# An encoder block whose up-projection weight sums are made ahead for ten of twenty-two channels instead of all

## The chip, the core and the metric

The kernel runs on one core of one Trainium2 chip. The metric is the device time of one launch in microseconds (us), the median of three runs. A profiled execution gives the trace. The engines are TensorE (PE, with its weight loads as PEld), VectorE (DVE), ScalarE (ACT), GpSimd (POOL) and SyncE (SP), which here issues every transfer from one queue.

## What is computed

Two sequences of 512 tokens, width 1024, all float32, go through one layer:

```python
h = _rmsnorm(x, g_attn) * (1 + sc1) + sh1
z = h @ w_in                        # q, k, v of mixer A; low-rank q, kv of mixer B; two gates
oa = _window_attention(qa, ka, va, sink_a)          # mixer A: window of +-128, 8 heads on 2 kv heads
# mixer B: dense attention, 8 heads, low-rank q and kv
mix = jax.nn.sigmoid(gla) * (oa @ w_o_a) + jax.nn.sigmoid(glb) * (ob @ w_o_b)
x = x + gt1 * (mix @ w_out)
h2 = _rmsnorm(x, g_ffn) * (1 + sc2) + sh2
u = _dwconv(h2 @ w_up, conv_w, conv_b)              # D_FF = 2816, so w_up is 1024 x 5632
ua, ug = jnp.split(u, 2, axis=-1)
x = x + gt2 * ((jax.nn.silu(ug) * ua) @ w_down)
```

## The kernel before

Each float32 operand of a matmul is split in two float32r parts, `hi` (a cast) and `lo` (the operand minus `hi`), and a product is three matmuls: hi by hi, hi by lo, lo by hi. One engine casts and the same or another subtracts; the subtraction reads two tensors from SBUF. Instructions stand on each engine in an order that a scheduler writes out when the program is built, and an engine takes them in that order: an instruction that waits holds all behind it. `tc.keep_in_program_order` pins an instruction of a helper among its engine's others.

The program's stages are: projections and preparation (0 to 225 us); the two attention mixers, B first and then A, with the gate projections filled in between (225 to 600); the output projection with the gated sum (600 to 800); the up-projection with convolution and gating (807 to 1215); the down-projection (to the end).

**Mixers.** A list of 128 units, 64 of mixer B (`PairB`) and then 64 of mixer A (`GroupA`), is walked in steps. A step issues the scores of one unit and five matmuls of the gate projection (`fill(5)`, `psg` in L495), and three steps later the transposes of that unit's softmax rows. The softmax (L530 to L540) goes DVE maximum, ACT exponential, DVE reciprocal, POOL scaling by `l` (L539); PE transposes the scaled `p` (L545). POOL also splits the gate weights (`wg`). A finished gate tile is copied by ACT to `go` (two buffers) and stored to `gate_d`.

**Weight sums.** The up-projection multiplies the two sequences with a Strassen-like scheme. `w_up` comes in 22 channels, each of four quarters, 128 x 512, which are called a1, a2 (the first half of the rows) and g1, g2 (the second half) here. Seven products per channel are made with the weights a1, a2, g2 and four sums of quarters. `weight_sums` runs one piece per step of the mixers: it loads half a channel (`wsum`, 512 KB, two buffers, L514), makes four POOL additions (L522 to L526) and stores the four sums to `su_d` in memory (L528). There are 44 such pieces, three steps each, over both mixers.

**Up-projection loop.** For each channel, `wraw` loads a quarter or a stored sum (256 KB, seven buffers, L764); `split_w` (L956 to L960) casts on ACT (L958) and subtracts on DVE or POOL (L959) into `wt` (eight buffers). The seven products are 12 matmuls each (L980), in the order a1 by `h1` into px; a2 by `h2` into pz; then the sums into px (`t2`), py (`t1`), px (`t3`), py (`e2`); and g2 into px (`t4`). ACT copies px after the first product and after `t2` and `t3`, and py after `t1` (L985); a product that adds to a bank waits for the copy of what was in it. `conv1` runs one ACT instruction (L991) and two on DVE (L992, L994) into `tmp_u`, four times a channel; `gated` (L999 to L1001) stores the result to `g_d`. The first convolution of a channel writes a `tmp_u` whose last content must have landed in `g_d`. SP issues loads and these stores in one order.

Of the kernel before, what the change touches and what calls it, by code (L numbers as in the profile page):

```python
# [8 lines left out]
F32 = mybir.dt.float32  # L9
# [9 lines left out]
S = 512  # L19
# [12 lines left out]
GW = 4 * AD + 2 * AD  # L32
FF = 2816
NP = FF // 128
EPS = 1e-6
BIG = -1e30

# [2 lines left out]
def encoder_block(ctx, tc, x, c_t, w_ada0, b_col, w_ada, b_ada, cols, w_z, w_g, gains, tabs, sink,  # L40
                  w_uq, w_ukv, w_o, w_out, w_up, conv, w_down, out):
    nc = tc.nc
    V, A, G, PE, SY = nc.vector, nc.scalar, nc.gpsimd, nc.tensor, nc.sync
# [7 lines left out]
    o_d = dram.tile([NB, 8, 128, S], F32, name="o_d")  # L51
    g_d = dram.tile([NB, NP, 128, S], F32, name="g_d")
    x1_d = dram.tile([TOK, D], F32, name="x1_d")
    gt_d = dram.tile([2, NB, D], F32, name="gt_d")
    su_d = dram.tile([NP, 128, 4, 512], F32, name="su_d")

# [5 lines left out]
    a1 = const.tile([128, KD, NB], F32, name="a1")  # L62
    a2 = const.tile([128, KD, NB], F32, name="a2")
# [5 lines left out]
    def split_pool(hi, lo, raw, in_order=False):  # L69
        ins = G.tensor_scalar(out=hi, in0=raw, scalar1=1.0, scalar2=0.0, op0=ALU.mult, op1=ALU.add)  # L70
        if in_order:
            tc.keep_in_program_order(ins)
        G.tensor_sub(lo, raw, hi.bitcast(F32))  # L73
# [21 lines left out]
    def mean_eps(a, ss, n):  # L95
        V.tensor_scalar(out=a, in0=ss, scalar1=1.0 / n, scalar2=EPS, op0=ALU.mult, op1=ALU.add)

# [21 lines left out]
    def hblk(name, shape=None, dt=F32R):  # L119
        return hp.tile(shape or [128, KD, S], dt, name=name, tag="h")  # L120
# [7 lines left out]
    with ExitStack() as st:  # L128
# [184 lines left out]
        with ExitStack() as s0:  # L313
# [140 lines left out]
            for _ in mods:  # L454
                pass

    mp = ctx.enter_context(tc.tile_pool(name="mp", bufs=1))

    def mblk(name, tag, shape=None, dt=F32R):
        return mp.tile(shape or [128, KD, S], dt, name=name, tag=tag, bufs=2)  # L460


    with ExitStack() as st:
        gw = st.enter_context(tc.tile_pool(name="gw", bufs=1, side="right"))
# [6 lines left out]
        def gates():  # L471

            ws = []

            def load():
                n = len(ws)
                if n < 2 * KD:
                    w = gw.tile([128, 2, KD, 128], F32R, name="wg", bufs=3)
                    raw = gw.tile([128, KD, 128], F32, name="wg_raw", bufs=2)
                    SY.dma_start(raw, w_g[n // 2, :, n % 2])  # L480
                    for k in range(0, KD, 4):
                        split_pool(w[:, 0, k:k + 4], w[:, 1, k:k + 4], raw[:, k:k + 4])
                    ws.append(w)

            load()
            load()
            for n in range(2 * KD):
                f, m = divmod(n, 2)
                for b in range(NB):
                    if b:  # L490
                        load()
                    ps = psg.tile([128, S], F32, name="psg")
                    for k in range(KD):
                        for i, (wl, hl) in enumerate(((0, h_hi), (0, h_lo), (1, h_hi))):
                            PE.matmul(ps, lhsT=ws[n][:, wl, k, :], rhs=hl[b][:, k, :],  # L495
                                      start=k == 0 and i == 0, stop=k == KD - 1 and i == 2)
                            yield
                    go = gw.tile([128, S], F32, name="go", bufs=2)
                    A.copy(go, ps)
                    SY.dma_start(gate_d[b, f, :, m], go)  # L500

        def weight_sums():

            pin = tc.keep_in_program_order
            halves = [(c, slice(256 * q, 256 * (q + 1))) for c in range(NP) for q in range(2)]
            ts = {}

            def load(n):  # L510
                if n < len(halves):
                    c, cs = halves[n]
                    ts[n] = gw.tile([128, 4, 256], F32, name="wsum", bufs=2)
                    pin(SY.dma_start(ts[n], w_up[c].rearrange("m q p n -> p (m q) n")[:, :, cs]))  # L514

            load(0)
            yield
            yield
            for n, (c, cs) in enumerate(halves):
                t = ts[n]  # L520
                load(n + 1)
                pin(G.tensor_add(t[:, 3], t[:, 2], t[:, 3]))  # L522
                pin(G.tensor_sub(t[:, 2], t[:, 0], t[:, 2]))
                yield
                pin(G.tensor_sub(t[:, 0], t[:, 3], t[:, 0]))
                pin(G.tensor_sub(t[:, 1], t[:, 1], t[:, 0]))  # L526
                yield
                pin(SY.dma_start(su_d[c, :, :, cs], t))  # L528
                yield

        def softmax(ps, n, plen):

# [86 lines left out]
        for j in range(2):  # L619
            n = 1 - 2 * j  # L620
# [91 lines left out]

        blocks = [PairB(b, g) for b in range(NB) for g in range(BH // 2)] + [GroupA(b, g) for b in range(NB) for g in range(AKV)]
        gate = gates()
        wsum = weight_sums()

        def fill(n):
            for _ in range(n):
# [43 lines left out]
    def wraw(src):  # L762
        r = wp.tile([128, 512], F32, name="wraw", bufs=7)
        SY.dma_start(r, src)  # L764
        return r

    def wtile():
        return wp.tile([128, 2, 512], F32R, name="wt", bufs=8)
# [17 lines left out]
    with ExitStack() as s0:  # L786
        wk = s0.enter_context(tc.tile_pool(name="wko", bufs=2))
        ob = []
        raws = [mblk("o_raw0", "st", dt=F32), hblk("o_raw1", dt=F32)]
# [63 lines left out]
    with ExitStack() as s0:  # L853
        wk = s0.enter_context(tc.tile_pool(name="wkx", bufs=1))

        def tmp(tag):
            return wk.tile([128, S], F32, name=f"tmp_{tag}", bufs={"cc": 6, "sf": 4}.get(tag, 2))
# [94 lines left out]

        cw = wk.tile([128, 2 * NP, 4], F32, name="cw")
        SY.dma_start(cw, conv)

        def split_w(raw, lo_eng):  # L956
            w = wtile()
            A.copy(w[:, 0], raw)  # L958
            lo_eng.tensor_sub(w[:, 1], raw, w[:, 0].bitcast(F32))  # L959
            return w.rearrange("p a (k n) -> p a k n", k=4)  # L960

        def weights_first(c):
            for q in range(2):
                yield split_w(wraw(w_up[c, 0, q]), G)

        def weights_rest(c):

            for q, eng in ((0, V), (3, V), (2, V), (1, G)):
                yield split_w(wraw(su_d[c, :, q]), eng)
            yield split_w(wraw(w_up[c, 1, 1]), G)  # L970

        def weights_all(c):
            yield from weights_first(c)
            yield from weights_rest(c)

        def product(ps, w, name, add=False, sl=slice(0, S)):
            for i in range(4):
# [10 lines left out]
        def conv1(c, m, src):  # L988
            cc = c + m * NP
            u = tmp(f"u{m}")  # L990
            A.activation(u, src, AF.Identity, scale=cw[:, cc, 1:2], bias=cw[:, cc, 3:4])  # L991
            V.scalar_tensor_tensor(out=u[:, 1:S], in0=src[:, 0:S - 1], scalar=cw[:, cc, 0:1], in1=u[:, 1:S],  # L992
                                   op0=ALU.mult, op1=ALU.add)
            V.scalar_tensor_tensor(out=u[:, 0:S - 1], in0=src[:, 1:S], scalar=cw[:, cc, 2:3], in1=u[:, 0:S - 1],  # L994
                                   op0=ALU.mult, op1=ALU.add)
            return u
# [54 lines left out]

        for c in range(NP):
            if c < EARLY:
                rest(c, weights_rest(c), *started[c])
            else:
                w = weights_all(c)
                if c == NP - 1:
                    rest(c, w, *first(w), [lambda k=k: down_step(0, k) for k in (1, 2)])
                else:
                    rest(c, w, *first(w))  # L1060
                if c == NP - 2:
                    down_step(0, 0)


    with ExitStack() as s0:
        wk = s0.enter_context(tc.tile_pool(name="wke", bufs=2))
        LATE = 3
        for b in range(NB):
# [22 lines left out]
            for i in range(NT):  # L1091
                t = b * NT + i
                xt = wk.tile([128, D], F32, name="xe", bufs=3)
                SY.dma_start(xt, x1_d[t * 128:(t + 1) * 128, :])
                for hf in range(2):
                    products(i, NP - LATE, NP, (hf,))
                    cs = slice(hf * 512, (hf + 1) * 512)
# [71 lines left out]
```

## Time and profile before

| | |
|---|---|
| median of 3 runs | 1458.52 us (1457.64 to 1461.35) |
| profiled execution, its own time | 1463.69 us |
| its span, first to last instruction | 1461.9 us |
| PE busy | 1395.4 us, 95% of the span |
| DVE, ACT, POOL busy | 64%, 46%, 42% |
| memory read, written | 186.67 MB, 67.13 MB |
| mean granted TensorE clock | 0.989 |

A matmul of 128 x 512 is recorded with about 389 ns but issues every 227 ns, since they are pipelined; busy time is that of the union. The granted clock is a share of full speed. An idle time is put down to what ended it.

### The profile page before, as it was taken

The numbers are of one execution on the slowest core, as the hardware profiler recorded it, in microseconds if no ns is written. First come the engines' busy times: TensorE is split into PE (matmuls) and PEld (weight loads), VectorE is DVE, ScalarE is ACT, GpSimd is POOL, SyncE is SP. The second block draws the span as 40 slices with busy tenths as digits, with TensorE's granted clock in tenths as the row PEclk, the third lists the DMA queues.
The fourth block names the chain that finished last, engine by engine and source line by source line (L and its number), as shares of the span: only waits on it lengthen the run. The fifth ranks groups of instructions, "written<-read, shape, count | busy, mean of one in ns | idle before, by whom it ended". The sixth has DMA issues, their size and how long they took to land.

```text
span 1461.9 us, 21179 instructions
## 1 busy us (share of the span) xinstructions
PE 1395.4 (95%) x7184; PEld 1155.7 (79%) x7184; DVE 941.7 (64%) x1885; ACT 679.5 (46%) x1385; POOL 609.0 (42%) x702
## 2 busy tenths in 40 slices
PE   5888997999999899999998999999999999999998
PEld 4777776888878787787887888888888887888887
DVE  4788774666668786564369776666666668347433
ACT  3475223666666566332136765555555554212210
POOL 3175023676677787455003232222222235444430
PEclk9999999999999999999999999999999999999999
DMA  8565764666666667855432344444434447646522
GB/s 320 195 209 178 239 234 159 196 227 202 227 198 220 208 212 250 286 174 177 143 115 80 108 130 130 125 127 123 130 123 127 132 122 250 205 140 222 185 80 72
DMA packets 162620, 255.19 MB, mean 175 GB/s; under 512 B 21192, under 2 KB 86984, under 8 KB 159440
## 3 DMA queue, kind: packets, MB, share of 16 engines
q1 hardware_dynamic: 162512, 253.84, 53.2%
q8 instruction: 57, 0.93, 0.3%
q14 instruction: 51, 0.42, 0.1%
HBM read 186.67 MB, written 67.13 MB: 174 GB/s over the span
## 4 chain that ended last, share of the span: by engine, by line
PE 78%; DVE 10%; DMA 5%; POOL 3%; ACT 2%; issue 2%; SPq 0%; ACTq 0%; POOLq 0%; DVEq 0%
PE px L980 15%; PE psg L495 9%; PE py L980 8%; PE psd L80 5%; PE psd L81 5%; PE psd L82 5%; PE pz L980 4%; PE ppt L545 3%; PE ppo L608 2%; PE psx L82 2%; PE psx L81 2%; PE psx L80 2%; PE psz L80 1%; PE psz L82 1%; PE psz L81 1%
## 5 line engine op out<-in xcount | busy, mean ns | idle before, releaser
L959 POOL TENSOR_TENSOR wt<-wraw,wt 128x512 fp32r<-128x512 f32 x88 | 119.4, 1363 | 395.4 <-ACT wt L958 362.9
L980 PE MATMUL px<-t,wt 128*128 128x512 f32 x792 | 190.0, 389 | 1.7 <-ACT tmp_cc L985 1.7
L980 PEld LDWEIGHTS px<-t,wt 128*128 128x128 f32 x792 | 148.5, 188 | 33.1 <-ACT tmp_cc L985 2.4
L495 PE MATMUL psg<-h_hi,wg 128*128 128x512 f32 x512 | 172.1, 401 | 0.0
L77 DVE TENSOR_TENSOR wd<-wraw,wd 128x512 fp32r<-128x512 f32 x88 | 96.3, 1133 | 90.8 <-ACT wd L76 90.8
L80 PE MATMUL psd<-wd 128*128 128x512 f32 x352 | 137.0, 389 | 0.1
L82 PE MATMUL psd<-wd 128*128 128x512 f32 x352 | 136.9, 389 | 0.0
L81 PE MATMUL psd<-wd 128*128 128x512 f32 x352 | 136.9, 389 | 0.0
L76 ACT CAST wd<-wraw 128x512 fp32r<-128x512 f32 x88 | 50.8, 619 | 151.5 <-issue 112.7
L958 ACT CAST wt<-wraw 128x512 fp32r<-128x512 f32 x154 | 93.9, 619 | 39.7 <-POOL wt L959 26.5
L495 PEld LDWEIGHTS psg<-h_hi,wg 128*128 128x128 f32 x512 | 97.0, 192 | 18.7 <-POOL wg L73 0.8
L539 POOL TENSOR_SCALAR p<-p,l 128x512 f32<-128x512 f32 (+2 forms) x128 | 78.3, 615 | 63.7 <-DVE l L538 45.9
L495 PE MATMUL psg<-h_lo,wg 128*128 128x512 f32 x256 | 102.7, 401 | 0.0
L537 ACT ACTIVATE p<-pps,nm 128x512 f32<-128x512 f32 (+2 forms) x128 | 78.1, 610 | 39.2 <-DVE nm L534 31.3
L992 DVE SCALAR_TENSOR_TENSOR tmp_u<-tmp_cc,cw,tmp_u 128x511 f32<-128x511 f32 x66 | 57.2, 867 | 41.5 <-ACT tmp_u L991 41.4
L70 POOL TENSOR_SCALAR wd<-wraw 128x512 fp32r<-128x512 f32 x44 | 33.6, 764 | 112.5 <-PE psd L82 84.9
L80 PEld LDWEIGHTS psd<-wd 128*128 128x128 f32 x352 | 66.1, 188 | 14.3 <-issue 0.5
L82 PEld LDWEIGHTS psd<-wd 128*128 128x128 f32 x352 | 66.1, 188 | 13.8
L81 PEld LDWEIGHTS psd<-wd 128*128 128x128 f32 x352 | 66.1, 188 | 13.5
L534 DVE TENSOR_REDUCE nm<-pps 128x1 f32<-128x512 f32 (+2 forms) x128 | 74.7, 584 | 3.2 <-PE pps L82 1.5
L545 PE MATMUL ppt<-ident,p 128*128 128x128 f32 x416 | 66.9, 274 | 8.2 <-POOL p L539 8.2
L73 POOL TENSOR_TENSOR wd<-wraw,wd 128x512 fp32r<-128x512 f32 x44 | 73.1, 1661 | 3.7
(256 smaller groups left out, 3425.7 us busy)
## 6 DMA issues: line engine op xcount, KB each, us to landing
w_ada<-in_w_ada_dram SPq DMA_DIRECT2D x24, 1024.0 KB, 5.5
wsum<-in_w_up_dram SPq DMA_DIRECT2D x44, 512.0 KB, 3.9
su_d<-wsum SPq DMA_DIRECT2D x44, 512.0 KB, 3.6
wraw<-su_d SPq DMA_DIRECT2D x88, 256.0 KB, 3.1
wraw<-in_w_down_dram SPq DMA_DIRECT2D x88, 256.0 KB, 3.2
wraw<-in_w_up_dram SPq DMA_DIRECT2D x66, 256.0 KB, 2.7
g_d<-tmp_u SPq DMA_DIRECT2D x44, 256.0 KB, 2.4
wraw<-g_d SPq DMA_DIRECT2D x44, 256.0 KB, 3.5
```

What stands on the lines that cost most here:

```text
L77: V.tensor_sub(lo, raw, hi.bitcast(F32))
L80: PE.matmul(ps, lhsT=lh, rhs=rh, start=first, stop=False)
L81: PE.matmul(ps, lhsT=lh, rhs=rl, start=False, stop=False)
L82: PE.matmul(ps, lhsT=ll, rhs=rh, start=False, stop=last)
L495: PE.matmul(ps, lhsT=ws[n][:, wl, k, :], rhs=hl[b][:, k, :], start=k == 0 and i == 0, stop=k == KD - 1 and i == 2)
L534: V.tensor_reduce(nm, ps[:, :n], op=ALU.max, axis=AX.X, negate=True)
L537: A.activation(p[:, :n], ps[:, :n], AF.Exp, bias=nm, accum_out=l)
L539: G.tensor_scalar(out=p[:, :plen], in0=p[:, :plen], scalar1=l, scalar2=1.0, op0=ALU.mult, op1=ALU.mult)
L545: PE.transpose(pt[:, j * 128:(j + 1) * 128], p[:, j * 128:(j + 1) * 128], ident)
L958: A.copy(w[:, 0], raw)
L959: lo_eng.tensor_sub(w[:, 1], raw, w[:, 0].bitcast(F32))
L980: PE.matmul(ps[:, sl], lhsT=w[:, wl, i], rhs=h[:, hl, sl], start=not add and i == 0 and n == 0, stop=i == 3 and n == 2, skip_group_check=add)
```

## The change

The sums of the first ten channels (`SUMMED = 10`) are still made during the mixers, in 20 pieces of three steps; there are three `wsum` buffers instead of two, and a piece's store is issued after the additions of the next piece. The second `go` buffer is gone. For the channels 10 to 21 no sum is made ahead or stored: the loop loads a2, g1, g2 beside a1, and POOL makes the four sums in SBUF from them (`tmp_sf`, four buffers that exist already), one channel at a time; DVE subtracts for all four (before: for three, POOL for the fourth).

```diff
+    quarters = [(c, 128 * q) for c in range(SUMMED) for q in range(4)]
+    def weight_sums(tile, width, count, ahead):
...
+        while n < len(loaded):
+            t, dst = loaded[n]
+            n += 1
+            load()
+            pin(G.tensor_add(t[:, 3], t[:, 2], t[:, 3]))
+            pin(G.tensor_sub(t[:, 2], t[:, 0], t[:, 2]))
+            yield
+            pin(G.tensor_sub(t[:, 0], t[:, 3], t[:, 0]))
+            pin(G.tensor_sub(t[:, 1], t[:, 1], t[:, 0]))
+            yield
+            if summed:
+                pin(SY.dma_start(*summed))
+            summed = (dst, t)
+            yield
...
-                    go = gw.tile([128, S], F32, name="go", bufs=2)
+                    go = gw.tile([128, S], F32, name="go", bufs=1)
...
-        wsum = weight_sums()
+        wsum = weight_sums(lambda: gw.tile([128, 4, 256], F32, name="wsum", bufs=3), 256, 2 * SUMMED, 1)
...
+        def weights_rest(c, raws=None):
+            if c < SUMMED:
+                for q, eng in ((0, V), (3, V), (2, V), (1, G)):
+                    yield split_w(wraw(su_d[c, :, q]), eng)
+                yield split_w(wraw(w_up[c, 1, 1]), G)
+                return
+            a1, a2 = raws
+            g1, g2 = wraw(w_up[c, 1, 0]), wraw(w_up[c, 1, 1])
+            sf = [tmp("sf") for _ in range(4)]
+            G.tensor_add(sf[0], g1, g2)
+            G.tensor_sub(sf[1], sf[0], a1)
+            yield split_w(sf[1], V)
+            yield split_w(sf[0], V)
+            G.tensor_sub(sf[2], a1, g1)
+            yield split_w(sf[2], V)
+            G.tensor_sub(sf[3], a2, sf[1])
+            yield split_w(sf[3], V)
+            yield split_w(g2, G)
```

The rows below are the built program's order, engine by engine; line numbers differ between the two files (L539 is L554 after the change, L764 is L779, L959 is L974, L1001 is L1032). POOL at the start of mixer A, before:

```order
L539 TENSOR_SCALAR p<-p,l 128x512 x3
L522 TENSOR_TENSOR wsum<-wsum 128x256
L523 TENSOR_TENSOR wsum<-wsum 128x256
L539 TENSOR_SCALAR p<-p,l 128x512
L525 TENSOR_TENSOR wsum<-wsum 128x256
L526 TENSOR_TENSOR wsum<-wsum 128x256
L70 TENSOR_SCALAR wg<-wg_raw 128x512 x2
L73 TENSOR_TENSOR wg<-wg_raw,wg 128x512
L539 TENSOR_SCALAR p<-p,l 128x256
L73 TENSOR_TENSOR wg<-wg_raw,wg 128x512
```

and the same place after the change:

```order
L554 TENSOR_SCALAR p<-p,l 128x512 x4
L71 TENSOR_SCALAR wg<-wg_raw 128x512 x2
L74 TENSOR_TENSOR wg<-wg_raw,wg 128x512
L554 TENSOR_SCALAR p<-p,l 128x256
L74 TENSOR_TENSOR wg<-wg_raw,wg 128x512
L554 TENSOR_SCALAR p<-p,l 128x384 x2
```

The additions no longer stand between the scalings; the gate weights' splits still do. POOL has no other rows in the mixers that differ in kind.

POOL in the loop at a late channel, where before it held `wt` subtractions alone (82 in a row, four per channel), after the change:

```order
L991 TENSOR_TENSOR tmp_sf<-wraw 128x512
L992 TENSOR_TENSOR tmp_sf<-tmp_sf,wraw 128x512
L995 TENSOR_TENSOR tmp_sf<-wraw 128x512
L997 TENSOR_TENSOR tmp_sf<-wraw,tmp_sf 128x512
L974 TENSOR_TENSOR wt<-wraw,wt 128x512 x3
```

The four sums are those of one channel; the three subtractions behind them are g2 of the channel before it and a1, a2 of the channel itself. POOL's instructions per channel go from four to seven.

SP in the loop at a late channel, one channel's period, before:

```order
L764 DMA wraw<-in_w_up_dram 128x512
L764 DMA wraw<-su_d 128x512 x4
L764 DMA wraw<-in_w_up_dram 128x512 x2
L1001 DMA g_d<-tmp_u_10761 128x512
L1001 DMA g_d<-tmp_u_10808 128x512
```

and after:

```order
L779 DMA wraw<-in_w_up_dram 128x512 x4
L1032 DMA g_d<-tmp_u_10914 128x512
L1032 DMA g_d<-tmp_u_10958 128x512
```

Four loads stand between two channels' stores instead of seven. PE's order is the same in both programs.

## Rows read from the trace of the kernel before

**Rows 1.** Busy time by stretch: start:end, length, PE, PEld, DVE, ACT, POOL (instructions), PE clock, DMA share, GB/s.

```profile
225.00:430.00 205.00, 202.01 (x1065) 167.99 (x1064) 129.42 (x258) 124.33 (x265) 130.56 (x178) 0.99 0.61 201
430.00:592.00 162.00, 151.88 (x832) 127.77 (x832) 122.98 (x371) 99.83 (x259) 120.65 (x179) 0.98 0.69 223
600.00:612.00 12.00, 9.69 (x40) 7.46 (x41) 5.81 (x8) 6.60 (x11) 4.72 (x5) 1.00 0.94 347
815.00:1187.00 372.00, 372.00 (x1642) 308.00 (x1641) 246.06 (x329) 210.06 (x344) 106.43 (x80) 1.00 0.44 131
```

**Rows 2.** PE's waits, 425 to 612 us: who waited for whom, total, times, longest.

```profile
PE ppt L545 <- POOL p L539: 8.2, 5, 3.4
PE ppo L608 <- ACT p L547: 1.5, 1, 1.5
PE psy L82 <- POOL wo L73: 0.9, 1, 0.9
PE psy L80 <- POOL wo L70: 0.8, 1, 0.8
PE psy L80 <- POOL wo L73: 0.8, 1, 0.8
```

**Rows 3.** Chain that ended last, near 490 us: start, duration, what.

```profile
485.53 0.74 POOL wsum L526
...
486.28 3.37 DMA su_d<-wsum
...
489.66 5.93 DMA wsum<-in_w_up_dram
...
497.23 0.49 POOL p L539
...
497.76 0.44 PE ppt L545 x2
```

**Rows 4.** The same chain near 432 us and from 575 us on.

```profile
431.94 5.62 DMA lda<-qa_d
...
575.86 4.81 DMA wsum<-in_w_up_dram
...
589.44 3.84 DMA o_d<-o
...
593.35 2.82 DMA wo_raw<-in_w_o_dram
...
601.48 7.24 DMA wo_raw<-in_w_o_dram
```

**Rows 5.** Busy time by stretch behind the two longest waits (columns of Rows 1).

```profile
498.60:502.10 3.50, 3.50 (x13) 3.00 (x12) 2.02 (x7) 0.49 (x2) 2.13 (x4) 0.51 1.06 388
...
583.90:587.40 3.50, 3.50 (x13) 3.02 (x12) 0.42 (x1) 1.41 (x3) 3.26 (x5) 0.51 0.44 150
```

**Rows 6.** DMA issues in mixer A, 430 to 592 us: count, KB each, median us to landing.

```profile
su_d<-wsum SPq DMA_DIRECT2D x23, 512.0 KB, 3.9
wsum<-in_w_up_dram SPq DMA_DIRECT2D x22, 512.0 KB, 3.7
...
gate_d<-go SPq DMA_DIRECT2D x15, 256.0 KB, 4.2
```

**Rows 7.** Tile `go` in the same stretch: ns min/median/max, first and last start.

```profile
L499 ACT COPY go<-psg x15: 576/587/598, 433.5 to 588.9; 128x512 f32<-128x512 f32 x15
...
DMA to landing us min/median/max: 3.3/4.2/8.3
```

**Rows 8.** The loop near 911 us in order of time: start, duration, engine, line, what [idle before].

```profile
910.95 2.88 PE L980 MATMUL px<-h,wt 128*128 128x512 f32 x12
...
921.83 2.88 PE L980 MATMUL px<-t,wt 128*128 128x512 f32 x12
...
913.27 1.35 POOL L959 TENSOR_TENSOR wt<-wraw,wt 128x512 fp32r<-128x512 f32 x1 [2.81 <-ACT wt L958]
916.49 1.29 POOL L959 TENSOR_TENSOR wt<-wraw,wt 128x512 fp32r<-128x512 f32 x1 [1.86 <-ACT wt L958]
...
914.05 1.13 DVE L994 SCALAR_TENSOR_TENSOR tmp_u<-tmp_cc,cw,tmp_u 128x511 f32<-128x511 f32 x1
...
919.79 0.75 DVE L994 SCALAR_TENSOR_TENSOR tmp_u<-tmp_cc,cw,tmp_u 128x511 f32<-128x511 f32 x1
920.46 0.69 DVE L959 TENSOR_TENSOR wt<-wraw,wt 128x512 fp32r<-128x512 f32 x1
...
915.81 1.18 SPq L1001 DMA_DIRECT2D g_d<-tmp_u  x2
...
918.16 0.82 ACT L991 ACTIVATE tmp_u<-tmp_cc,cw 128x512 f32<-128x512 f32 x1 [0.91 <-DMA g_d<-tmp_u]
```

**Rows 9.** The last channel: PE's wait, then SP's and ACT's rows before it.

```profile
PE px L980 <- ACT tmp_cc L985: 1.7, 1, 1.7
...
1205.90 0.93 SPq L1001 DMA_DIRECT2D g_d<-tmp_u  x2
...
1208.00 0.81 ACT L991 ACTIVATE tmp_u<-tmp_cc,cw 128x512 f32<-128x512 f32 x1 [2.58 <-DVE wd L77]
```

**Rows 10.** A DVE instruction between two of POOL, near 871 us.

```profile
870.78 1.78 DVE L994 SCALAR_TENSOR_TENSOR tmp_u<-tmp_cc,cw,tmp_u 128x511 f32<-128x511 f32 x1
```

More of the change, by code (lines that the diff above doesn't have):

```diff
@@ L34 @@
 NP = FF // 128
+SUMMED = 10
 EPS = 1e-6
@@ L455, in encoder_block, with load @@
                 pass
+    quarters = [(c, 128 * q) for c in range(SUMMED) for q in range(4)]
+    def weight_sums(tile, width, count, ahead):
+        pin = tc.keep_in_program_order
+        loaded = []
+        def load():
+            if len(loaded) < count and quarters:
+                c, c0 = quarters[0]
+                del quarters[:width // 128]
+                t, cs = tile(), slice(c0, c0 + width)
+                pin(SY.dma_start(t, w_up[c].rearrange("m q p n -> p (m q) n")[:, :, cs]))
+                loaded.append((t, su_d[c, :, :, cs]))
+        for _ in range(ahead):
+            load()
+        yield
+        yield
+        n, summed = 0, None
+        while n < len(loaded):
+            t, dst = loaded[n]
+            n += 1
+            load()
+            pin(G.tensor_add(t[:, 3], t[:, 2], t[:, 3]))
[3 more added lines that the diff above has]
+            pin(G.tensor_sub(t[:, 1], t[:, 1], t[:, 0]))
+            yield
+            if summed:
+                pin(SY.dma_start(*summed))
+            summed = (dst, t)
+            yield
+        if summed:
+            yield
+            yield
+            pin(SY.dma_start(*summed))
     mp = ctx.enter_context(tc.tile_pool(name="mp", bufs=1))
@@ L497, in gates @@
                             yield
-                    go = gw.tile([128, S], F32, name="go", bufs=2)
+                    go = gw.tile([128, S], F32, name="go", bufs=1)
                     A.copy(go, ps)
                     SY.dma_start(gate_d[b, f, :, m], go)
[L504 to L529, printed above, removed]
         def softmax(ps, n, plen):
@@ L964, in weights_first @@
                 yield split_w(wraw(w_up[c, 0, q]), G)
[L966 to L970, printed above, removed]
+        def weights_rest(c, raws=None):
[16 more added lines that the diff above has]
+            yield split_w(g2, G)
         def weights_all(c):
-            yield from weights_first(c)
-            yield from weights_rest(c)
+            raws = (wraw(w_up[c, 0, 0]), wraw(w_up[c, 0, 1]))
+            for r in raws:
+                yield split_w(r, G)
+            yield from weights_rest(c, raws)
         def product(ps, w, name, add=False, sl=slice(0, S)):
```

## The prediction

> **What bounds the kernel now.** I read the busy shares first, then the busy time stage by stage, and then PE's waits in each stage. PE is busy 95% of the span and its order is the same in both programs, so only PE's idle time and its time at half clock can change. The table by stretch [rows 1] is to be read by length minus PE busy. Mixer B loses 205.00 − 202.01 = 3.0 us, mixer A 162.00 − 151.88 = 10.1 us, and 372 us of the up-projection's loop nothing. So the two places that the change touches differ: in mixer A there is something to win, in the loop only something to lose. There DVE works 246 and POOL 106 of the 372 us.
>
> PE's waits of mixer A come next [rows 2]: 8.2 us in five waits on POOL's scaling of `p`, two of them some 3.4 us long. At the first transposes of `p` (437 us) stand 1.5 us more. From 592 to 612 us three waits on the splits of `wo` make 0.9 + 0.8 + 0.8 = 2.5 us.
>
> What POOL was doing is in the chain of waits [rows 3]. The last addition of a piece ends at 486.27. Its store then takes 3.37 us, the next load into the same of two `wsum` buffers 5.93 us (to 495.59), and only then do POOL's two additions run and the scaling behind them, at 497.23, which PE's transposes at 497.76 wait for. POOL's scaling has its exponentials by then: it is stuck in order, behind additions that wait for their load. The second long wait has the same form, with a load of 4.81 us [rows 4].
>
> The waits cost twice. Behind each, PE ran 3.50 us at a granted clock of 0.51 [rows 5], which is the 1.2 GHz level of its two, after it had stood idle 3.4 us. At full clock that work takes 0.51 × 3.5 = 1.8 us, so each wait costs another 1.7 us, 3.4 in all.
>
> **The change part by part.**
>
> *No sums in mixer A.* The 24 pieces of channels 10 to 21 go, with 24 loads, 24 stores and 96 POOL additions of some 0.74 us [rows 3]; nearly all of them lie in this stretch. The order rows of mixer A show scalings with no addition between them. The two long waits go, 2 × 3.35 = 6.7 us, if nothing else is late by as much. Next in line at those places are the splits of `wg`, which stay on POOL ahead of scalings; they make waits under 1 us (of the 8.2, 1.5 us stand outside the two long ones), and of that 1.5 I count 0.7 gained. Of the 3.4 us of half clock I count 3.0, since what is left of the short waits may still bring some.
>
> *Less traffic beside the other transfers.* The DMA share is 0.69 in mixer A and 0.94 from 600 to 612 us [rows 1]. There `lda` takes 5.62 us, `o_d` 3.84, the next `wo_raw` loads 2.82 and 7.24 [rows 4]; the last stands in SP's order behind `gate_d` and `su_d` stores. Without the 23 stores and 22 loads of 512 KB of the sums [rows 6] (23.6 MB, two thirds of the 36 MB that 223 GB/s moves in 162 us) these run nearer their fastest. Of the 1.5 us at `lda` I count 1.0 and of the 2.5 us at `wo` 1.8; the bounds are nothing and the whole.
>
> *Mixer B: third buffer, late store.* The sums' rate stays (a piece in three steps), and no wait on sums stands there to gain: 3.0 us idle in all. A store a piece later frees its buffer later, but there is a third. Nothing, either way; a miss would look like [rows 3] and cost 3.4 + 1.7 = 5 us each.
>
> *One `go` buffer.* ACT's next copy of a gate tile waits until the store has landed. The 15 copies from 433.5 to 588.9 us come 155.4 / 14 = 11.1 us apart on average, and their stores land in 3.3 to 8.3 us [rows 7], so nothing is added as long as the copies keep their distance. At the end of the mixers the store stands behind loads of `o` and `wo_raw`; there ACT may wait for it. It is busy 6.6 of 12 us [rows 1], so I put that at nothing for PE.
>
> *Twelve channels summed in the loop.* The channel's period is 19.04 us, given by PE. POOL's instructions go from four to seven per channel, each of two SBUF inputs and 128 x 512 like the splits of 1.29 to 1.35 us [rows 8]: 7 × 1.32 = 9.3 us of 19, where it was 106.43 / 372 × 19.04 = 5.4. DVE takes one split more, 0.69 us: 246 / 372 × 19.04 = 12.6 becomes 13.3 us. ACT's casts stay. The loads fall from seven to four per channel, and the stored sums' loads go. Each engine still has 5 us to spare in a channel; what hides the additions is that they are made a channel ahead of PE's use of them. If that cover went, a channel would lose what POOL adds, 3 × 1.32 = 4.0 us.
>
> The tight path is another: the products `t2`, `t3` on one side, ACT's copies and the convolution on the other. In [rows 8] the store of `g_d` is issued at 915.81; it has landed when ACT's convolution starts at 918.16, and `t3` starts at 921.83. In the last channel [rows 9], where the store was issued late, ACT starts at 1208.00 and PE can go on 1.34 us later, after its copy. So in a normal channel PE has 921.83 − 918.16 − 1.34 = 2.33 us in hand. The store hangs on DVE's last operations of the channel before. These are what POOL disturbs: L994 takes 0.75 us alone, 1.13 beside a POOL split [rows 8], and 1.78 between two of them [rows 10]. A POOL instruction thus holds DVE by 0 to 1.03 us; the nearest row to the usual meeting is 1.13, so 0.4. With three more per channel that is 0 to 3.1 us, by my value 1.2, and not all of it before the store. That is below 2.33. I put the loop at 0.5 us in all, between 0 and the slower rival below.
>
> The Trainium skill speaks against this part. Its page "SBUF — State Buffer", section "Who interferes with whom", calls the ports that DVE and GpSimd share an exclusive lock, so that a second instruction waits for the first to end. The rows agree in kind: 1.78 is 0.75 plus most of a POOL instruction. By the rule at its worst each of the three added instructions would hold DVE for its length, 3 × 1.32 = 4.0 us, which is past the slack; by the row of 1.13, 1.2 us, which is not.
>
> *Change-over, channel 9 to 10.* Four additions stand ahead of channel 9's last splits on POOL: 0 to 1 us, I take 0.3.
>
> *Last channel.* Its 1.7 us wait [rows 2, 9] comes from a store issued only at 1205.90, behind loads that waited for buffers. Now its four quarters are loaded a channel earlier and no others follow: 1.4 of 1.7 gained.
>
> **Sum.** Gains 6.7 + 0.7 + 3.0 + 1.0 + 1.8 + 1.4 = 14.6; losses 0.5 + 0.3 = 0.8; net 13.8. From the profiled execution's 1463.7 that gives 1449.9. That execution is 5.2 us above the median, longer than any of the three runs, so its waits on transfers may be longer than usual ones; I take 12.5 off the median: 1446.0. With every wait named here gone, 6.7 + 1.5 + 3.4 + 1.5 + 2.5 + 1.7 = 17.3, it is 1441; with the uncertain terms at nothing, some 8.5, it is 1450.
>
> **Rivals.** A change under 0.3% (4.4 us) could not be told from none here.
>
> *Half the gain (1452).* POOL in mixer A is busy 120.65 of 162 us with the sums; 96 × 0.74 = 71 us of that goes, which speaks against POOL as the next bound. For it speaks that DVE, at 123 of 162 us, stands ahead of every scaling in the softmax, and that `wg` splits keep their place. If each long wait becomes one of 1.7 us with half of the half-clock, 5.0 of the gain stays away, and if nothing is won at `wo` another 1.8: 1446 + 6.8 = 1453, about 1452.
>
> *No change (1455 to 1458).* PE reaches the end of the mixers 10 us earlier, but the last loads and stores there (`o_d`, `wo_raw`) arrive when they did, or ACT's single `go` buffer delays them; the gain returns as a wait at 600 us. The DMA share of 0.94 speaks for it; that much of it was stores of sums speaks against.
>
> *Slower (1465).* In the late channels DVE is held by POOL so that the `g_d` store comes later than the 2.33 us in hand. At 4.0 us late (the exclusive case) a channel loses 4.0 − 2.33 = 1.7 us, twelve lose 20; 1458.5 − 13 + 20 = 1465. It decides from 2.33 + 13 / 12 = 3.4 us late. Against it: DVE has 5.7 us free per channel, and the waiting chain starts afresh in each.
>
> **Chances.** Forecast 0.66, half the gain 0.15, no change 0.10, slower 0.09. Faster by over 0.3% is the first two, less a little where the second ends above 1454: 0.80; the same 0.11; slower 0.09. The forecast's own range is 1441 to 1450. To leave out no more than 2 in 10 the range takes in the second case and the lower end of the third: 1441 to 1456.
>
> **What would show it.** Right: no PE wait over 1 us on the scaling of `p` after 437 us, no half-clock stretch near 500 and 585 us, mixer A some 10 us shorter, PE still without idle time in the late channels, the last channel's wait under 0.5 us. Wrong: waits on `p` that name `wg` splits or DVE's maximum ahead of them (second case); a new wait on `wo` or `go` near 590 us (third); PE waits on `tmp_cc` once per channel from channel 10 on, ending on the `g_d` store or on L994 at over 1.5 us (fourth). The last would make the forecast wrong by most.

## The result, and the profile after

The changed kernel takes 1448.47 us (median of four runs, 1447.74 to 1448.98), the kernel before 1458.64 on the same chip: a ratio of 0.9927 (95% interval 0.991 to 0.9944), 10 us faster. The forecast was 1446.0 with a range of 1441 to 1456. The profiled execution took 1448.04 us, 15.65 less than that of before.

Busy time by stretch after the change, with the columns of [rows 1]: mixer B, mixer A until PE ends the gate projection, the start of the output projection, early channels, the change-over from stored to fresh sums, late channels.

```profile
225.00:425.00 200.00, 199.84 (x1068) 166.64 (x1067) 129.43 (x251) 125.38 (x266) 129.74 (x175) 1.00 0.60 199
425.00:579.00 154.00, 153.03 (x852) 130.01 (x851) 123.30 (x370) 99.10 (x258) 60.97 (x94) 1.00 0.28 96
579.00:612.00 33.00, 27.17 (x110) 22.00 (x110) 17.68 (x23) 11.79 (x17) 10.53 (x10) 0.90 0.66 227
795.00:950.00 155.00, 155.00 (x685) 128.41 (x684) 109.19 (x146) 91.51 (x152) 42.92 (x32) 1.00 0.42 129
950.00:975.00 25.00, 24.78 (x109) 20.20 (x109) 20.41 (x22) 13.65 (x22) 17.82 (x12) 1.00 0.31 92
1000.00:1180.00 180.00, 180.00 (x796) 149.05 (x795) 132.21 (x162) 99.35 (x163) 86.28 (x65) 1.00 0.27 85
```

Mixer A now loses 1.0 us where it lost 10.1, at full clock. But the 33 us behind it lose 5.8 us, at a mean clock of 0.90. PE's waits from 425 to 612 us say what they are; beside [rows 2] all waits on POOL's `p` and on `wo` are gone, and one new wait stands there, whose releaser the view doesn't name:

```profile
PE psy L81 <- issue: 5.8, 1, 5.8
PE ppo L623 <- DVE p L563: 0.5, 1, 0.5
```

ACT's rows in order of time at that place, then SP's, then the landing times of the `go` stores from 566 to 590 us:

```profile
574.09 0.59 ACT L543 COPY go<-psg 128x512 f32<-128x512 f32 x1 [4.92 <-PE psg L539]
583.56 1.14 ACT L77 CAST o<-o_raw 128x512 fp32r<-128x512 f32 x2 [8.88 <-DMA o_raw<-o_d]
584.60 0.58 ACT L543 COPY go<-psg 128x512 f32<-128x512 f32 x1
```

```profile
573.81 0.38 SPq L806 DMA_DIRECT2D o_raw<-o_d  x1
574.70 0.33 SPq L544 DMA_DIRECT2D gate_d<-go  x1
```

```profile
DMA to landing us min/median/max: 2.2/2.8/9.5
```

PE ended the gate projection at 579.45. The last gate copy runs only at 584.60 and ends at 585.18; PE starts the output projection at 585.28 (its row is below). The `go` buffer which that copy needs is held by the store issued at 574.70, behind the 2 MB load of `o`, and this store landed 9.5 us later, at 584.2. In the built order the copy also stands behind two casts that wait for the same load. PE's first matmul of `psy` takes a PSUM bank only when that copy has emptied the gate projection's bank; the program's order of waits says this, the trace only that the times fit. Behind the wait PE runs at half clock; of these 7 us it is busy for 4.72:

```profile
583.00:590.00 7.00, 4.72 (x11) 3.77 (x12) 5.56 (x8) 6.41 (x11) 2.67 (x2) 0.51 0.91 329
```

### The profile page after: what moved, and what is told of

The parts are those of the page before. It is cut to its first block, busy times and chain, and to the rows that moved or that the text cites. A ratio compares the mean times of both kernels' runs of the same rounds, so it can differ in the third digit from the quotient of the medians.

```text
span 1446.2 us, 20961 instructions
## 1 busy us (share of the span) xinstructions
PE 1391.7 (96%) x7184; PEld 1155.8 (80%) x7184; DVE 971.5 (67%) x1897; ACT 679.0 (47%) x1385; POOL 591.9 (41%) x642
## 4 chain that ended last, share of the span: by engine, by line
PE 80%; DVE 12%; ACT 2%; POOL 2%; issue 2%; DMA 1%; SPq 0%; ACTq 0%; DVEq 0%; POOLq 0%
PE px L1011 15%; PE psg L539 10%; PE py L1011 8%; PE psd L81 5%; PE psd L82 5%; PE psd L83 5%; PE pz L1011 4%; PE ppt L560 3%; PE ppo L623 2%; PE psx L83 2%; PE psx L82 2%; PE psx L81 2%; PE psz L81 2%; PE psy L81 1%; PE psy L83 1%
## 5 line engine op out<-in xcount | busy, mean ns | idle before, releaser
L974 POOL TENSOR_TENSOR wt<-wraw,wt 128x512 fp32r<-128x512 f32 x76 | 105.8, 1400 | 284.4 <-ACT wt L973 276.0
L539 PE MATMUL psg<-h_hi,wg 128*128 128x512 f32 x512 | 170.3, 398 | 0.0
L554 POOL TENSOR_SCALAR p<-p,l 128x512 f32<-128x512 f32 (+2 forms) x128 | 78.9, 618 | 125.1 <-DVE l L553 66.6
L539 PEld LDWEIGHTS psg<-h_hi,wg 128*128 128x128 f32 x512 | 96.1, 190 | 18.5 <-POOL wg L74 0.8
L539 PE MATMUL psg<-h_lo,wg 128*128 128x512 f32 x256 | 101.9, 398 | 0.0
L1023 DVE SCALAR_TENSOR_TENSOR tmp_u<-tmp_cc,cw,tmp_u 128x511 f32<-128x511 f32 x66 | 66.1, 1002 | 40.3 <-ACT tmp_u L1022 40.3
L973 ACT CAST wt<-wraw 128x512 fp32r<-128x512 f32 x106 | 64.1, 616 | 33.3 <-PE py L1011 17.7
L83 PEld LDWEIGHTS psd<-wd 128*128 128x128 f32 x352 | 66.1, 188 | 13.8
L1022 ACT ACTIVATE tmp_u<-tmp_cc,cw 128x512 f32<-128x512 f32 x66 | 53.7, 813 | 38.0 <-DMA g_d<-tmp_u 26.0
```

Source lines behind the costliest of these rows:

```text
L83: PE.matmul(ps, lhsT=ll, rhs=rh, start=False, stop=last)
L539: PE.matmul(ps, lhsT=ws[n][:, wl, k, :], rhs=hl[b][:, k, :], start=k == 0 and i == 0, stop=k == KD - 1 and i == 2)
L554: G.tensor_scalar(out=p[:, :plen], in0=p[:, :plen], scalar1=l, scalar2=1.0, op0=ALU.mult, op1=ALU.mult)
```

## Where the 15.65 us lie

PE's order is the same in both programs, so the same instruction's start in both traces gives a running balance. PE's rows of before at four marks, the end of the preparation, the first matmuls of the output projection, of the up-projection and of the down-projection:

```profile
223.94 0.90 PE L159 MATMUL psa<-ident,br 128*128 128x128 f32 x3 [5.00 <-DVE br L156]
...
600.56 0.47 PE L80 MATMUL psy<-o,wo 128*128 128x512 f32 x1 [0.77 <-POOL wo L73]
...
786.58 0.50 PE L980 MATMUL px<-h,wt 128*128 128x256 f32 x2 [0.36 <-ACT wt L958]
...
1217.64 0.39 PE L80 MATMUL psd<-wd 128*128 128x512 f32 x1
```

and of after:

```profile
220.34 0.90 PE L160 MATMUL psa<-ident,br 128*128 128x128 f32 x3 [4.75 <-DVE br L157]
...
585.28 0.76 PE L81 MATMUL psy<-o,wo 128*128 128x512 f32 x1 [5.83 <-issue]
...
770.76 0.50 PE L1011 MATMUL px<-h,wt 128*128 128x256 f32 x2 [0.35 <-ACT wt L973]
...
1201.25 0.39 PE L81 MATMUL psd<-wd 128*128 128x512 f32 x1
```

PE is ahead by 3.60, then 15.28, 15.82 and 16.39 us, and 15.7 at the end (spans 1461.9 and 1446.2). The first 3.60 lie in the preparation, which the change doesn't touch. Between the first two marks 11.68 us are gained after the new wait has taken 5.06 (5.83 − 0.77), so the mixers alone gave 16.7. PE's first score matmul of mixer A starts at 429.8 us before and at 422.9 after, 6.9 us apart: 3.3 of the 16.7 lie in mixer B, whose waits come and go (run 5), and 13.4 in mixer A. The output projection gives 0.5, the loop 0.6, and the end takes 0.7 back. Without the preparation and mixer B it is 8.8 us, near the 10 us between the medians.

## The experiments

Twelve runs follow, in four groups: nine variants, one of them twice, and the changed kernel twice more. Each group ran on one chip together with the kernel before, and all ratios are to that. A size "over the change" is taken from the changed kernel of the same group where one ran there, else from its ratio of 0.993.

**1. The last gate tiles in idle buffers.** The changed kernel; its `wsum` buffers are free by then.

```diff
-                    go = gw.tile([128, S], F32, name="go", bufs=1)
+                    if n < 2 * KD - 4:
+                        go = gw.tile([128, S], F32, name="go", bufs=1)
+                    else:
+                        go = gw.tile([128, 4, 256], F32, name="wsum", bufs=3)[:, 0:2].rearrange("p a n -> p (a n)")
```

> The changed kernel with one edit: the last eight gate tiles are copied into the wsum buffers, which are idle by then, so that a gate copy no longer waits for the store of the one before. Theory A (the single go buffer makes the new wait of 5.83 us at 579 us and the 6.83 us of half clock behind it, 9.2 us together): the last gate copy stands ahead of the casts of o again, PE waits under 1 us at the first matmul of the output projection, no half clock there, and the time is 1448.5 - 9 = 1439 to 1441 us. Rival B (the loads of o and wo_raw come no earlier whatever happens, and PE would wait for them instead): a wait of 4 us or more stays within 10 us of that place, under another name, and the time is 1446 to 1449 us.

Measured: 0.989 (0.9871 to 0.9908). PE's waits from 425 to 615 us:

```profile
PE psy L81 <- issue: 0.7, 1, 0.7
PE ppo L626 <- DVE p L566: 0.5, 1, 0.5
```

The wait is gone and no rival took its place within 10 us, so theory A holds for the cause. The size is smaller than the 9 us expected: against the changed kernel's 0.993 it is 0.4%, 6 us. The traces agree: from the first score matmul of mixer A to the first matmul of the output projection, PE takes 162.4, 161.9 and 162.1 us in the three traces of the change, and 157.2, 157.2 and 157.3 us here and in runs 4 and 6, 5 us less. The half clock was overrated: the expectation counted 6.83 us of it, of which PE was busy for 4.72, and from that matmul to the up-projection PE takes 185.5 us in the change against 184.6 here and 183.9 and 185.8 in runs 4 and 6, so little of it is left. Here waits of 1.3 and 1.1 us on the splits of `wo` near 655 us are followed by 3.4 us of half clock.

**2. The kernel before with one `go` buffer.**

```diff
-                    go = gw.tile([128, S], F32, name="go", bufs=2)
+                    go = gw.tile([128, S], F32, name="go", bufs=1)
```

> The kernel before with one edit: one go buffer instead of two, all sums still made ahead. Theory A: the last gate copy falls behind two casts that wait for the 2 MB load of o; PE, which reached the output projection at 599.8 us, waits until after 605.5 us, some 5 us, then runs at half clock for 3 to 7 us; about 1.7 us of the waits on wo are covered by it. Time 1458.6 + 5 to 9 = 1464 to 1468 us. Rival B (the wait comes from the loads, which are there anyway): 1458 to 1460 us, no new wait.

Measured: 1.0041 (1.0021 to 1.0061), 6 us slower than before. Its waits from 425 to 615 us:

```profile
PE ppt L545 <- POOL p L539: 7.7, 5, 3.5
PE psy L80 <- issue: 7.4, 1, 7.4
PE ppo L608 <- ACT p L547: 1.8, 1, 1.8
```

The new wait appears without any other part of the change, and POOL's waits stay. The single buffer alone makes it.

**3. All 22 channels summed ahead, with the change's buffers and late store.**

```diff
-SUMMED = 10
+SUMMED = 22
```

> The changed kernel with SUMMED = 22: all sums made ahead as in the kernel before, but with three wsum buffers and the store a piece behind, and one go buffer; no sums in the loop. Theory P (the two long waits in mixer A came from POOL being stuck behind the load of its next piece, whose buffer the store held): with the load issued a piece earlier than the store needs, POOL no longer waits for wsum and the waits on p of 3.4 us are gone though all the traffic stays; against the kernel before with one go buffer it gains 8 to 10 us, so it comes to some 1455 to 1459 us. Rival Q (the sums have to leave mixer A, since their traffic or their POOL time is the limit): waits of 3 us on p stay, and it comes within 2 us of the kernel before with one go buffer.

Measured: 0.997 (0.9954 to 0.9986), against 1.0041 for run 2: 10 us gained with every sum still in the mixers. The waits, same stretch:

```profile
PE psy L81 <- issue: 7.2, 1, 7.2
PE ppt L560 <- POOL p L554: 3.5, 3, 2.5
PE ppo L623 <- DVE p L563: 0.5, 1, 0.5
```

Of 7.7 us on `p`, 3.5 stay. So theory P is mostly right: POOL was held by loads that came late, not by a lack of time (it is busy 128.33 us of 163 in that mixer A). From mixer A's first score matmul to the output projection PE takes 169.6 us, against 176.8 in run 2: 7.2 us less. Moving the sums out takes the rest. Which of the two, the third buffer or the late store, does it was not run.

**4. Ten channels ahead, two `wsum` buffers, prompt store, two `go` buffers.**

```diff
-            if summed:
-                pin(SY.dma_start(*summed))
-            summed = (dst, t)
+            pin(SY.dma_start(dst, t))
...
-                    go = gw.tile([128, S], F32, name="go", bufs=1)
+                    go = gw.tile([128, S], F32, name="go", bufs=2)
...
-name="wsum", bufs=3
+name="wsum", bufs=2
```

> The changed kernel with ten channels summed ahead, but with the buffers of the kernel before: two wsum buffers, each piece stored right after its additions, and two go buffers. Theory A with the prediction's step on mixer B (the third buffer and the late store bring nothing there): the time is that of the changed kernel with spare go buffers, 1439 to 1441 us, and PE waits in mixer B for no sums. Rival M (mixer B needs the third buffer at this pace): waits of 3 us on p in mixer B, each some 5 us with its half clock, and 1444 us or more.

Measured: 0.9878 (0.9856 to 0.9899). PE's waits in mixer B (225 to 425 us), none of them on sums, and from 425 to 615 us:

```profile
PE ppt L597 <- DMA ldb<-qb_d: 1.8, 1, 1.8
PE pps L81 <- ACT p L550: 1.5, 1, 1.5
...
PE psy L81 <- issue: 0.8, 1, 0.8
PE ppo L621 <- DVE p L561: 0.5, 1, 0.5
```

So the third buffer and the late store bring nothing once the sums are out of mixer A: run 1, which has them and no wait on `go`, comes to 0.989, within the interval. In the change they stand beside a single `go` buffer; whether both would fit was not run. This kernel beats the kernel before and the changed one.

**5. The changed kernel again, and once more in the last group of runs.**

> The changed kernel itself, to stand beside the two other kernels of this row and for a second trace. Theory A (single go buffer): the wait at the first matmul of the output projection recurs at 5 to 7 us with 7 us of half clock behind it. If that wait was a chance of one execution, it is under 2 us. The waits on ldb (1.7 us) and on ACT's exponential (1.3 us) in mixer B, which the kernel before showed and the changed one did not, are expected to come and go between executions whatever the kernel. Ratio to the kernel before 0.991 to 0.995.

> The changed kernel again, on the chip of the next run. Ratio to the kernel before 0.991 to 0.995.

Measured: 0.9934 (0.9914 to 0.9955) and 0.9934 (0.9907 to 0.996). The new wait recurs, 5.4 and 5.5 us. So do the two waits of mixer B, which the first trace of the change had lacked but for 0.2 us: 1.7 on `ldb` and 1.7 on ACT's `p` in the former. They are no effect of the change.

**6. Run 4's kernel beside the changed one.**

> Ten channels summed ahead with two wsum buffers, prompt store and two go buffers, once more beside the changed kernel on one chip. If the single go buffer is the step that failed, it is 5 to 8 us faster than the changed kernel; if the earlier difference came from the chip, within 3 us.

Measured: 0.9894 (0.9869 to 0.992) beside 0.9934; medians 1448.84 and 1454.04, 5.2 us apart. That is at the lower end of what was expected, and with the intervals overlapping this group alone wouldn't settle it; run 4's whole interval lies below the first one of the change, and the traces above show the same 5 us.

**7. Four channels ahead instead of ten** (run 4's kernel, `SUMMED = 4`).

> Four channels summed ahead instead of ten, two wsum buffers, prompt store and two go buffers: 18 channels are summed in the loop, and mixer B loses most of its sums. Theory L (a summed channel costs the loop nothing once it runs, and mixer B has nothing to win from the sums): the ratio to the kernel before is that of the same kernel with ten channels, 0.988, within 0.002. Rival S: each of the six further channels costs 0.5 us or more, ratio 0.990 or more. Rival T (traffic and POOL's work of the sums delay mixer B and the stages beside it): ratio under 0.986.

Measured: 0.9925 (0.9905 to 0.9944), 0.005 worse than run 4: the number that rival S expected, but not its reason. Against the repeat of that kernel in run 6, 0.9894, it is 0.003 with overlapping intervals, so the size of the loss is not sure. From 900 to 1180 us PE is busy all of 280.00 us, so a running late channel costs nothing. What the trace shows of a loss in the loop is at the change-over, which now comes early: two waits there, 800 to 930 us,

```profile
PE px L1009 <- ACT tmp_cc L1014: 3.4, 2, 2.3
```

and 1.7 us on ACT's `p` in mixer B and 2.8 us on `wo` in this execution, whose cause is open.

**8. The sums of a late channel made twice** (11 POOL instructions per channel).

```diff
             G.tensor_add(sf[0], g1, g2)
+            G.tensor_add(sf[0], g1, g2)
             G.tensor_sub(sf[1], sf[0], a1)
+            G.tensor_sub(sf[1], sf[0], a1)
...
             G.tensor_sub(sf[2], a1, g1)
+            G.tensor_sub(sf[2], a1, g1)
...
             G.tensor_sub(sf[3], a2, sf[1])
+            G.tensor_sub(sf[3], a2, sf[1])
```

> The changed kernel, each of the four sums of a late channel made twice on POOL: 11 POOL instructions per channel, some 14.5 of 19.04 us. Theory L (DVE is held by some 0.4 us per POOL instruction, and PE has over 2 us in hand): DVE's busy time in a late channel rises from 14.3 to 15.5 to 16 us, the period of a channel stays at 19.04 us and the time is that of the changed kernel within 2 us. Rival S (the slower rival of the prediction: the held convolution makes the store of g_d late): PE waits for tmp_cc in every late channel, 0.5 to 2 us each, 6 to 24 us in all.

Measured: 1.0169 (1.0151 to 1.0187), 34 us slower than the change. Theory L falls for this load; the prediction's slower rival is real, only further out. Between PE's second products of successive channels (`pz`) the trace has 28.4 us at the change-over, 9.3 over the 19.04 of a running channel, and then 21.2 on average, 24.1 us over in eleven channels; three of these still take 19.04. PE's waits, 960 to 1215 us, and one channel in order of time:

```profile
PE px L1015 <- ACT tmp_cc L1020: 24.0, 9, 7.1
```

```profile
1056.89 3.49 DVE L1035 TENSOR_TENSOR tmp_u<-tmp_u,tmp_u 128x512 f32<-128x512 f32 x2
...
1058.70 2.03 SPq L1036 DMA_DIRECT2D g_d<-tmp_u  x2
...
1061.67 0.81 ACT L1026 ACTIVATE tmp_u<-tmp_cc,cw 128x512 f32<-128x512 f32 x1 [2.94 <-DVE wt L974]
...
1063.01 1.20 PE L1015 MATMUL px<-t,wt 128*128 128x512 f32 x4 [1.76 <-ACT tmp_cc L1020]
```

The two gating products take 3.49 us, the store is issued at 1058.70, ACT starts at 1061.67, and PE goes on 1.34 us later. (The view names DVE's split for ACT's wait. That ended at 1061.58; the store landed 2.9 us after its issue, at 1061.60, and it is the store that the convolution's `tmp_u` needs. From 1000 to 1180 us the view names the store in five of ACT's waits there, 13.7 us, and the split in two, 5.9.) The mean of a product on DVE, late channels of the change first, then of this run:

```profile
L1031 DVE TENSOR_TENSOR tmp_u<-tmp_u,tmp_u 128x512 f32<-128x512 f32 x18 | 12.3, 686 | 1.4 <-ACT tmp_u L1030 1.3
```

```profile
L1035 DVE TENSOR_TENSOR tmp_u<-tmp_u,tmp_u 128x512 f32<-128x512 f32 x16 | 25.7, 1641 | 0.2 <-ACT tmp_u L1034 0.2
```

**9. Two of the four sums made twice** (`sf[2]` and `sf[3]`; 9 POOL instructions).

> The changed kernel with two of the four sums of a late channel made twice: 9 POOL instructions per channel, between the 7 of the change and the 11 that lost 2 us per channel. Theory H2 (the loss sets in where POOL no longer waits between its instructions and its splits of the next channel meet the gating products): at 9, 11.9 of 19.04 us, POOL still waits, the period stays at 19.04 us outside the change-over channel, and the time is that of the changed kernel plus 0 to 3 us. Rival G (each added instruction costs a share): half the loss of 11, about 1 us per channel, 12 to 18 us in all.

Measured: 0.9973 (0.9957 to 0.9988), 6 us over the change. PE waits 6.1 us on `tmp_cc` in five waits, 3.8 of them at the change-over, and the gating products stay at 0.69 us. More than H2 allowed, less than G. In this trace the change-over takes 5.7 us over 19.04 and the eleven channels behind it 4.1 in all: the loss per running channel is not in proportion to the instructions (0 at 7, 0.4 us at 9, 2.2 at 11).

**10. Memsets in place of second sums:** four, then ten per channel. They write the tile that the sum then fills, and read nothing.

```diff
+            for _ in range(3):
+                G.memset(sf[0], 0.0)
             G.tensor_add(sf[0], g1, g2)
```

> The changed kernel with a POOL memset of 128 x 512 ahead of each of the four sums of a late channel: 11 POOL instructions per channel as in the run with the sums made twice, but the four added ones read nothing. Theory H (that run lost 2 us per channel because POOL's reading instructions held DVE's two-input ones, above all the gating products): DVE's busy time in a late channel stays within 0.5 us of the changed kernel's 14.3 us, the period stays at 19.04 us, and the time is that of the changed kernel within 3 us. Rival P (POOL itself was late: its chain of sums and splits does not fit): with memsets of 0.5 us or more the period grows as well, by the share of POOL's added time, 0.5 to 2 us per channel. If the memsets are far shorter than 1.3 us each, the run tells less and the text must say so.

Measured with four: 0.9905 (0.9877 to 0.9933); waits of 1.0 us on `tmp_cc`. A memset takes 0.53 us, so it tells little, as was foreseen, and DVE's busy time rose all the same, to 149.11 of 180 us.

> The changed kernel with ten POOL memsets of 128 x 512 ahead of the sums of a late channel (3, 2, 3, 2). At the 0.53 us that one took in the run with four, they add 5.3 us to POOL per channel, as much as the four second sums did (4 x 1.32), but they read nothing. Theory H (the loss with the sums made twice is DVE being held by POOL's reading instructions): the period stays near 19.04 us, PE's waits on tmp_cc in the late channels sum to under 6 us, and the time is that of the changed kernel within 4 us. Rival P (POOL's own lateness, whatever fills it): PE waits in most late channels as with the sums made twice, 24 us in all, and the ratio to the kernel before is over 1.01.

Measured with ten: 0.9984 (0.9966 to 1.0002), 7 us over the change, where the second sums cost 34. Late channels, 1000 to 1180 us, with ten memsets and then with the sums made twice:

```profile
1000.00:1180.00 180.00, 174.96 (x755) 141.79 (x754) 154.01 (x156) 92.81 (x155) 145.34 (x156) 0.99 0.28 85
```

```profile
1000.00:1180.00 180.00, 166.37 (x713) 135.16 (x712) 160.03 (x145) 86.23 (x144) 148.84 (x94) 0.98 0.25 75
```

POOL is about as busy in both (145 and 149 us), but PE loses 5.0 us in one and 13.6 in the other; on `tmp_cc` it waits 4.8 us from 955 to 1215 us, against 24.0. Part of the gap is the change-over, which takes 0.3 us over 19.04 with memsets and 9.3 with second sums; the eleven channels behind it lose 9.6 and 24.1 us. So over half of run 8's loss in running channels goes with instructions that read, and the rest comes with POOL's lateness whatever fills it.

The length of the gating products does not separate the two runs: with memsets they rose to 1.78 us, more than run 8's 1.64, and POOL's splits run beside them (splits from 1040.17 to 1045.31, products from 1042.39 to 1045.86), where in the change POOL stands idle (from 1014.73 to 1016.60 with the products from 1015.21). What differs is DVE's whole work in a channel (its share of the 180 us times the mean period there): 14.0 us in the change, 17.2 with memsets, 19.0 with second sums, which is all of PE's 19.04.

The time misses H's 4 us by 3. As POOL's work per channel differs too (16.2 and 17.7 us by the same reckoning), the two parts are not cleanly separated.

## Why the prediction was right, and where it was off

The place, the sign and the size class were right. By steps:

- **No sums in mixer A:** forecast 6.7 + 0.7 + 3.0 + 1.0 = 11.4, measured 13.4 in the trace's balance; the short waits on `p` went altogether, and no half clock stayed in mixer A. Run 3 qualifies the reason: POOL was stuck behind late loads, as [rows 3] showed, and a third buffer with a late store would have cured over half of the waits without moving a sum.
- **One `go` buffer:** this step failed. It was put "at nothing for PE". The 11.1 us between copies is a mean; the last ones stand closer (568.6 and 574.1 us, and PE was done with the next tile at 579.45), and the store between them stands behind the 2 MB load of `o`. The text had seen that ACT may wait there, and looked at ACT's share of busy time instead of asking which PSUM bank PE's next matmul needs. It costs 5.8 us of wait and, with 4.7 of 7.0 us PE-busy at 0.51, another 0.49 × 4.72 = 2.3 us; of these 8.1 us, 5 come back in the traces of runs 1, 4 and 6, and 5 to 8 between the medians; runs 1 and 2 make the wait go and come alone. The step on `wo`, forecast 1.8, can't show in the change, since the new wait covers the place; in runs 1 and 4, without that wait, no wait on `wo` is left up to 615 us. This is the prediction's third case, in part: a wait at the end of the mixers took back about a third of the gain, and the half clock near 585 us, whose absence was to show it right, is there from a new cause.
- **Mixer B:** nothing either way, as forecast (run 4).
- **Sums in the loop:** 0.5 + 0.3 forecast. In the late channels PE is busy 180.00 of 180.00 us; the change-over loses 0.5, 1.0 and 0.3 us in the three traces of the change (its channel takes 19.6, 20.0 and 19.3). POOL's 9.3 us are 86.28 / 180 × 19.04 = 9.1. DVE was 115.05 of 180 us in the same stretch of before,

```profile
1000.00:1180.00 180.00, 180.00 (x796) 149.07 (x794) 115.05 (x154) 99.37 (x162) 51.76 (x41) 1.00 0.43 128
```

  and is 132.21: (132.21 − 115.05) / 180 × 19.04 = 1.8 us more per channel. Without the added split of 0.7 that is 1.1 us of holding for three POOL instructions, 0.4 each as taken (0.4 and 0.5 in the other two traces). PE's slack of 2.33 us is now 2.06 by the same reckoning, from these rows of after: 1021.73 − 1018.33 − 1.34.

```profile
1018.33 0.82 ACT L1022 ACTIVATE tmp_u<-tmp_cc,cw 128x512 f32<-128x512 f32 x1 [1.17 <-DMA g_d<-tmp_u]
...
1021.73 1.52 PE L1011 MATMUL px<-t,wt 128*128 128x512 f32 x6
```

  The rule of the Trainium skill that was weighed there ("SBUF — State Buffer", section "Who interferes with whom", an exclusive lock between DVE and GpSimd) says what a meeting costs at most. Run 8 agrees: a product of 0.69 us takes 1.64 where it meets POOL, and DVE's work per channel rises from 14.0 to 19.0 us, 1.25 for each of four added instructions, which take 1.31 in the change. At seven instructions per channel POOL stands idle half of the time (86.28 of 180 us busy) and the products keep their 0.69 us, so the row's 0.4 was the better price there, not the rule's worst case.
- **Last channel:** 1.4 of 1.7 forecast; the wait on `tmp_cc`, which [rows 9] and not [rows 2] shows, is gone. In its place 0.6 us on DVE stands at 1210 us, at the start of the down-projection.

The median's 12.5 against 10.2 measured is thus one missed term, partly made up by larger gains than forecast. That they met so near the forecast is luck: run 4's kernel, which keeps two `go` buffers, gains 18.5 us and in run 6 16.5 between medians, more than the sum's 13.8, and the missed wait took the excess back. What 8.8 us of the balance leave of the 10 us between the medians isn't attributed.

## What to carry to other kernels

When memory is taken from one buffer to pay for another, price the donor at its worst place: there ask what its store queues behind, and whose PSUM bank waits for the copy into it. An engine stuck in order behind a late load looks like an engine with too much work; a piece more of prefetch tells the two apart before work is moved. Work on POOL beside a busy DVE can be free and still near an edge: two more instructions per channel than the change has cost 6 us, four more 34.

## What was not expected of the hardware

The cost of POOL beside DVE grows faster than the number of instructions. DVE's work in a channel is 12.2 us with four POOL instructions (before), 14.0 with seven, 16.6 with nine (153.28 of 180 us at a mean period of 19.5) and 19.0 with eleven. Without the added split, that is 0.4 us for each of the first three and about 1.3, a whole POOL instruction, for each further one. PE loses nothing at seven, 0.4 us per running channel at nine and 2.2 at eleven, where DVE's work fills PE's period. And a 256 KB store, one of 32 that land in 2.6 us at their median, took 9.5 us when issued 0.9 us behind a 2 MB load in the same queue.
